# RWKV chunk inverse: transpositions on VectorE and block products on TensorE in place of round trips through DRAM; squares and low parts moved in the opening

## The chip, the cores and the metric

The kernel runs on one core of one Trainium2 chip. The time is the device time of one execution, in microseconds (us). In what follows PE is TensorE (the matrix engine), DVE is VectorE, ACT is ScalarE, POOL is GpSimd and SP is SyncE, which here only issues DMAs. PEld is PE's loading of stationary operands, beside its matmuls.

## The reference

Two layers over 256 tokens of width 1024. Each layer is a half-step SwiGLU network, three token mixers side by side (differential attention, RWKV-7, HGRN2), whose outputs are gated and summed, and a second SwiGLU half-step. The part that the change touches is the RWKV recurrence, over 8 heads of width 64:

```python
def step(state, inp):
    r_t, w_t, k_t, v_t, kk_t, a_t = inp
    s_kk = jnp.einsum('bhvk,bhk->bhv', state, kk_t)
    state = (state * w_t[:, :, None, :]
             - s_kk[..., None] * (kk_t * a_t)[:, :, None, :]
             + v_t[..., None] * k_t[:, :, None, :])
    return state, jnp.einsum('bhvk,bhk->bhv', state, r_t)
```

and, at the very start, the first sub-layer's norm: `u = modulate(rms_norm(h, norm_w[l, 0]), m[0], m[1])`, where m comes from the conditioning vector through the matrix mod_w.

## The kernel before, in words

**Weights.** All projections read fp32 weights from HBM in tiles of 512 KB ("weight tiles" below). `load` brings one into `raw`, ACT rounds it to `wh` (L375), and DVE makes the rest `wl = raw - wh` (L376). Activations have such pairs too (uh and ul, zh and zl). A product is three matmuls: wh with the high half, wh with the low half, wl with the high half. `mm3` (L372) makes 24 matmuls of 256 columns from a tile; the projections whose rows are tokens make 12 of 512 (L952, L953, L954). wh and wl have three buffers each, raw four.

**Order.** The main loop goes through the weight tiles in a fixed list (`items`, ORDER, BUDGET). Before each tile `advance` steps through the "tracks", Python generators that issue the mixers' own work piece by piece: each `yield` names the cost of the piece, a negative one ends the track's turn for this tile. Within these bounds a scheduler sets the order of each engine's instructions at build time, by priorities (PRIO) and dependencies; `pin` keeps an instruction in the order of the program. An engine runs its list in order, and waits where the next instruction is not ready.

**RWKV.** Time is cut into four chunks (c) of 64 tokens, and in each the recurrence is solved with the inverse of a unit triangular 64x64 matrix, for 8 heads: 4 pairs (j) by 2 (p). `rwkv_pair` fills H with these matrices, s on partitions. `rwkv_rest` (before: L776) inverts all 32.
- It takes the two 32x32 blocks on each diagonal (q = 0, 1) and moves them through DRAM (scrA, L782 and L788) to lie one block to a partition: NT, 64 partitions, and a copy on the other 64.
- The recursion (L799 a product, L801 a sum, for t = 1 to 15) inverts the two 16x16 blocks in each at once, in the free dimension.
- Four operations over 2048 elements make the 16x16 block below the diagonal (L808, L811, L813, L816).
- The result Y returns through DRAM (scrY, L821 to L827) into Ys, with s on partitions again.
- DVE transposes the upper blocks (Xa, L837), and two rounds of small matmuls (L841, L847) make the 32x32 blocks off the diagonal.
- The loop over c follows: pR (L864), pU with the inverse in Ys (L873), the state pS (L882) and the output pO (L896, L900). The norm of the output begins at L917.

HGRN2's track runs beside it; its small matmuls are L1016 and its DVE products write hw and PX.

**Opening.** The first layer's norm and its first six weight tiles run tile by tile, t = 0 to 7 (L1358 to L1382): two `mw` tiles of mod_w come in and DVE reduces them (L324) to `modd` (L328) and `mods` (L340); ACT makes zf from h and modd (L1366), DVE copies two columns into it (L1367), `split` makes zh on ACT and zl on DVE, and PE multiplies what is there of zf with the first raw tiles in plain fp32 (L1376). The squares of h (`z_square`, ACT L420) are added up on POOL (acc, L422), and after t = 4 two matmuls sum them (L433) and DVE takes the reciprocal root (nst, L380 to L385). POOL also builds masks there (blk, lmf), for `constants`.

Of the kernel before, what the change touches and what calls it, by code (L numbers as in the profile page):

```python
# [63 lines left out]
def trunk(ctx: ExitStack, tc: tile.TileContext, A, out):  # L64
# [36 lines left out]
    id32 = cp.tile([128, 32], F32, name="id32")  # L101
    omu = cp.tile([128, L, 15], F32, name="omu")
# [21 lines left out]
    def constants():  # L124
# [26 lines left out]
        for i, n in enumerate(LV):  # L151
# [263 lines left out]
    def z_square(k):  # L415
# [4 lines left out]
        SC.activation(sq, h[k], AF.Square)  # L420
# [128 lines left out]
    scr = drp.tile([2, 2, 16, 32, 32], F32, name="scrA")  # L549
    scy = drp.tile([2, 2, 16, 32, 32], F32, name="scrY")  # L550
# [3 lines left out]
    def mixer(l):  # L554
# [218 lines left out]
        def rwkv_rest():  # L773
# [12 lines left out]
            TM = hp.tile([128, 2048], F32, name="TM", tag="ZH")  # L786
# [3 lines left out]
            GP.memset(Y.rearrange("m a b -> m (a b)")[:, 0:1024:33], 1.0)  # L790
            yield 0.1
# [11 lines left out]
            Yh = tile_([128, 8, 16], "Yh", "rnt")  # L803
            PT = tile_([128, 8, 16], "PT", "rny")
# [665 lines left out]
```

## Time and profile before

| | us |
|---|---|
| three runs, median (lowest to highest) | 1449.73 (1449.04 to 1454.76) |
| the profiled execution | 1454.69 |
| its span | 1453.0 |
| PE busy | 1401.6 (96%) |
| DVE busy | 1184.9 (82%) |
| ACT busy | 803.3 (55%) |
| POOL busy | 150.2 (10%) |
| start of the first L372 matmul, behind the opening | 50.33 |

PE's mean granted clock is 0.988 of full speed (1.0 is 2.4 GHz, 0.5 is 1.2 GHz). A line of the profile's groups reads: line of the kernel, engine, operation, output from inputs by their names in the program, shapes, count; then the busy time and the mean ns of one; then the idle time of the engine just before these instructions and what ended it. Matmul records of plain fp32 (not of the rounded halves) stand twice in the trace.

### The profile page before, as it was taken

What the parts mean: (1) busy time and instruction counts of PE and PEld (TensorE: products, weight loads), DVE (VectorE), ACT (ScalarE), POOL (GpSimd) and SP (SyncE); (2) the same over time, 40 slices, a digit from 0 to 9 for tenths busy, and PEclk for the clock granted to TensorE, in tenths of its full rate; (3) what the DMA queues carried; (4) which work ended last, traced back from release to release, by engine and by line L of the source; (5) the groups of instructions that cost most, each with busy time, mean ns of one, the idle gap of its engine ahead of it and who ended that gap; (6) DMA issues with size and microseconds to landing.
All of it is one profiled execution on the core that took longest, in us unless ns stands there. A gap on an engine that the chain in (4) does not pass through costs nothing. (4 is left out here: it accounts for less than half of the span.)

```text
span 1453.0 us, 31223 instructions
## 1 busy us (share of the span) xinstructions
PE 1401.6 (96%) x12420; PEld 1331.2 (92%) x12420; DVE 1184.9 (82%) x2216; ACT 803.3 (55%) x1374; POOL 150.2 (10%) x251
## 2 busy tenths in 40 slices
PE   4999999999899999999999999999989999999999
PEld 3899999998678899999999999999877789999998
DVE  5999988869679999888879898787797788886553
ACT  2575447874255646554545544588534664665542
POOL 6200010031310021000000000100322001100000
PEclk9999999999799999999999999999999999999999
DMA  9769984455415657899878998544552235665564
GB/s 358 264 241 362 322 311 167 146 160 163 130 60 178 201 183 264 291 332 319 303 251 296 351 344 299 191 143 144 182 165 78 76 129 174 202 220 192 198 194 127
DMA packets 90370, 316.51 MB, mean 218 GB/s; under 512 B 10608, under 2 KB 13040, under 8 KB 90224
## 3 DMA queue, kind: packets, MB, share of 16 engines
q1 hardware_dynamic: 86832, 308.84, 62.0%
q0 software_dynamic: 1600, 4.20, 1.1%
q8 instruction: 97, 1.59, 0.4%
q10 hardware_dynamic: 1792, 1.48, 0.4%
q14 instruction: 49, 0.40, 0.1%
HBM read 312.38 MB, written 2.10 MB: 216 GB/s over the span
## 5 line engine op out<-in xcount | busy, mean ns | idle before, releaser
L375 ACT CAST wh<-raw 128x1024 fp32r<-128x1024 f32 (+1 forms) x440 | 455.5, 1036 | 426.9 <-PE psd L372 237.3
L376 DVE TENSOR_TENSOR wl<-raw,wh 128x1024 fp32r<-128x1024 f32 (+1 forms) x440 | 537.2, 1222 | 110.7 <-ACT wh L375 106.6
L372 PE MATMUL psd<-uh,wl 128*128 128x256 f32 x1664 | 228.9, 279 | 6.5 <-DVE wl L376 6.5
L372 PE MATMUL psd<-uh,wh 128*128 128x256 f32 x1664 | 231.4, 280 | 0.0
L372 PE MATMUL psd<-ul,wh 128*128 128x256 f32 x1664 | 227.1, 278 | 0.0
L372 PEld LDWEIGHTS psd<-uh,wl 128*128 128x128 f32 x1664 | 207.2, 189 | 8.2 <-DVE wl L376 7.7
L372 PEld LDWEIGHTS psd<-uh,wh 128*128 128x128 f32 x1664 | 207.7, 188 | 5.0 <-issue 2.7
L372 PEld LDWEIGHTS psd<-ul,wh 128*128 128x128 f32 x1664 | 206.4, 188 | 0.4
L324 DVE SCALAR_TENSOR_TENSOR mw<-mw,cbc 128x1024 f32<-128x1024 f32 x134 | 168.2, 1257 | 1.7 <-DMA mw<-in_modw 1.6
L372 PE MATMUL psd<-hl,wh 128*128 128x256 f32 x704 | 96.8, 278 | 0.0
L372 PE MATMUL psd<-hh,wl 128*128 128x256 f32 x704 | 96.6, 278 | 0.0
L372 PE MATMUL psd<-hh,wh 128*128 128x256 f32 x704 | 96.3, 277 | 0.0
L422 POOL TENSOR_TENSOR acc<-acc,sq 128x256 f32<-128x256 f32 x36 | 31.1, 865 | 575.1 <-ACT sq L420 443.6
L372 PEld LDWEIGHTS psd<-hl,wh 128*128 128x128 f32 x704 | 87.9, 188 | 0.0
L372 PEld LDWEIGHTS psd<-hh,wl 128*128 128x128 f32 x704 | 87.9, 188 | 0.0
L372 PEld LDWEIGHTS psd<-hh,wh 128*128 128x128 f32 x704 | 87.7, 188 | 0.0
L953 PE MATMUL psd<-wl,uh 128*128 128x512 f32 x160 | 66.5, 416 | 3.8 <-DVE wl L376 3.8
L954 PE MATMUL psd<-wh,ul 128*128 128x512 f32 x160 | 67.3, 421 | 0.0
L952 PE MATMUL psd<-wh,uh 128*128 128x512 f32 x160 | 66.0, 414 | 0.0
L372 PE MATMUL psd<-zh,wh 128*128 128x258 f32 x448 | 65.2, 286 | 0.0
L372 PE MATMUL psd<-zh,wl 128*128 128x258 f32 x448 | 64.9, 283 | 0.0
L372 PE MATMUL psd<-zl,wh 128*128 128x258 f32 x448 | 63.9, 283 | 0.0
(428 smaller groups left out, 2032.3 us busy)
## 6 DMA issues: line engine op xcount, KB each, us to landing
raw<-in_gu SPq DMA_DIRECT2D x176, 512.0 KB, 4.7
mw<-in_modw SPq DMA_DIRECT2D x134, 512.0 KB, 5.5
raw<-in_wfm SPq DMA_DIRECT2D x94, 512.0 KB, 3.3
raw<-in_dn SPq DMA_DIRECT2D x64, 512.0 KB, 4.7
raw<-in_wtm SPq DMA_DIRECT2D x40, 512.0 KB, 3.3
raw<-in_dn SPq DMA_DIRECT2D x32, 384.0 KB, 4.4
raw<-in_wo SPq DMA_DIRECT2D x24, 512.0 KB, 3.3
raw<-in_wout SPq DMA_DIRECT2D x16, 512.0 KB, 3.3
```

Source lines behind the costliest of these rows:

```text
L324: ins = V.scalar_tensor_tensor(w, w, 1.0, NOW["cbc"], ALU.mult, ALU.mult, accum_out=modd[:, l, j, f:f + 1])
L372: PE.matmul(p, w[:, sl[k]], xs[k][x], start=first and i == 0, stop=last and i == 3 * n - 1)
L375: SC.copy(dst_h, src)
L376: V.tensor_sub(dst_l, src, dst_h.bitcast(F32))
L422: GP.tensor_add(NOW["acc"], NOW["acc"], sq)
L952: PE.matmul(ps[b], u[k][0][:, ts_], w1, start=k == 0, stop=False)
L953: PE.matmul(ps[b], u[k][0][:, ts_], w2, start=False, stop=False)
L954: PE.matmul(ps[b], u[k][1][:, ts_], w1, start=False, stop=k == KT - 1)
```

## The change

The inverse no longer leaves the chip. H's diagonal 32x32 blocks are gathered into Hd, block m of the four partition quarters side by side. DVE's transposition, which works on 32x32 blocks, puts the 16 matrices of a quarter and their two halves g on the 32 partitions (To). `half`, a new constant of two columns (1 on the first and on the last 16 of every 32 partitions), picks the right half of each: NT is one 16x16 block to a partition, on 128 partitions, and the recursion runs over one block instead of two. A second transposition brings the result back (Yd, masked by `half` into two diagonal blocks), a third gives Xa, and two rounds of 64 matmuls of 32x32 make the block off the diagonal (L831, L837 of the changed kernel). Ys is filled by four copies. The older two rounds follow as L849 and L856, with p now in the inner loop. The four operations over 2048 elements and all DMAs of scrA and scrY are gone.

In the opening the squares of tiles 2t-2 and 2t-1 are made at step t, behind zh, and pinned there; zl of tile t-1 is made at step t, behind the two copied columns of zf; z_sums takes sq ahead of acc.

```diff
+            if n == 16:
+                V.tensor_reduce(half[:, 0:1], lmf[:, 1], AX.X, ALU.max)
+                V.tensor_scalar(half[:, 1:2], half[:, 0:1], -1.0, 1.0, ALU.mult, ALU.add)
...
-        for i, sq in enumerate((NOW["acc"], NOW["sq"])):
+        for i, sq in enumerate((NOW["sq"], NOW["acc"])):
...
-            for q in range(2):
-                for p in range(2):
-                    r0 = 64 * p + 32 * q
-                    GP.dma_start(scr[q, p].rearrange("m s t -> s m t"),
-                                 H[r0:r0 + 32, :, :, 32 * q:32 * q + 32].rearrange("s j c t -> s (j c) t"))
-            NT = tile_([128, 32, 32], "NT", "r")
-            Y = tile_([128, 32, 32], "Y", "k")
-            for d in range(2):
-                GP.dma_start(NT[64 * d:64 * d + 64], scr.rearrange("q p m s t -> (q p m) s t"))
+            quad = [slice(32 * i, 32 * i + 32) for i in range(4)]
+            Hd = tile_([128, 16, 32], "Hd", "Xa")
+            for i, r in enumerate(quad):
+                (GP.tensor_copy if i % 2 else SC.copy)(
+                    Hd[r].rearrange("s (j c) t -> s j c t", j=4), H[r, :, :, 32 * (i % 2):32 * (i % 2) + 32])
+            NT = tile_([128, 16, 16], "NT", "r")
+            Y = tile_([128, 16, 16], "Y", "k")
+            V.transpose(To.rearrange("p t (g m) -> p t g m", g=2), Hd.rearrange("p m (g t) -> p t g m", g=2))
+            GP.memset(Bd[:, :, 0:16], 0.0)
+            SC.activation(Bd[:, :, 16:32], Hd[:, :, 16:32], AF.Copy, scale=half[:, 0:1])
+            SC.activation(NT, To[:, :, 0:16].rearrange("p t s -> p s t"), AF.Copy, scale=half[:, 0:1])
+            V.scalar_tensor_tensor(NT, To[:, :, 16:32].rearrange("p t s -> p s t"), half[:, 1:2], NT, ALU.mult, ALU.add)
...
             for t in range(1, 16):
-                tm = TM[:, 0:2 * t * t].rearrange("m (g j s) -> m g j s", g=2, j=t)
-                V.tensor_tensor(tm, ap(Y, 0, [[528, 2], [32, t], [1, t]]), ap(NT, t, [[528, 2], [0, t], [32, t]]),
-                                ALU.mult)
-                V.tensor_reduce(ap(Y, t, [[528, 2], [32, t]]), tm, AX.X, ALU.add)
-                yield 0.2 + 4 * t * t / 960.0
+                tm = TM[:, 0:t * t].rearrange("m (j s) -> m j s", j=t)
+                V.tensor_tensor(tm, ap(Y, 0, [[16, t], [1, t]]), ap(NT, t, [[0, t], [16, t]]), ALU.mult)
+                V.tensor_reduce(ap(Y, t, [[16, t]]), tm, AX.X, ALU.add)
+                yield 0.4 + 2.7 * t * t / 960.0
...
-            tm = TM.rearrange("m (j t s) -> m j t s", j=8, t=16)
-            V.tensor_tensor(tm, Yh.unsqueeze(2).to_broadcast([128, 8, 16, 16]),
-                            ap(NT, 16, [[0, 8], [1, 16], [32, 16]]), ALU.mult)
-            V.tensor_reduce(PT, tm, AX.X, ALU.add)
-            V.tensor_tensor(tm, PT.unsqueeze(2).to_broadcast([128, 8, 16, 16]),
-                            ap(Y, 528, [[0, 8], [1, 16], [32, 16]]), ALU.mult)
-            V.tensor_reduce(Yh, tm, AX.X, ALU.add)
...
-            GP.dma_start(sm[:, 0:8], Y[0:64, 0:8])
...
+            V.transpose(To.rearrange("p t (g m) -> p t g m", g=2),
+                        Y.rearrange("p s t -> p t s").unsqueeze(2).to_broadcast([128, 16, 2, 16]))
+            for g in range(2):
+                SC.activation(Yd[:, :, 16 * g:16 * g + 16], To[:, :, 16 * g:16 * g + 16].rearrange("p t m -> p m t"),
+                              AF.Copy, scale=half[:, g:g + 1])
+            V.transpose(Xa, Yd)
+            for m in range(16):
+                for i, r in enumerate(quad):
+                    PE.matmul(p1[r, m], Bd[r, m], Xa[r, m], start=True, stop=True, tile_position=(32 * i, 32 * i))
+            SC.copy(Tt, p1)
+            for m in range(16):
+                for i, r in enumerate(quad):
+                    PE.matmul(p2[r, m], Tt[r, m], Yd[r, m], start=True, stop=True, tile_position=(32 * i, 32 * i))
+            V.tensor_tensor(Yd[:, :, 16:32], Yd[:, :, 16:32], p2[:, :, 16:32], ALU.add)
+            for i, r in enumerate(quad):
+                (GP.tensor_copy if i % 2 else SC.copy)(Ys[r, :, 32 * (i % 2):32 * (i % 2) + 32], Yd[r])
+            V.transpose(Xa, Yd)
+            yield -1.0
...
-        split(zh[:, t], zl[:, t], zf[:, t])
+        if t:
+            pin(V.tensor_sub(zl[:, t - 1], zf[:, t - 1], zh[:, t - 1].bitcast(F32)))
+        SC.copy(zh[:, t], zf[:, t])
+        if 0 < t < 5:
+            for k in (2 * t - 2, 2 * t - 1):
+                z_square(k, pin)
...
-            for k in range(KT):
-                z_square(k)
```

Three places show how the instructions move. The first is DVE in the first layer, around the last steps of the inverse; the wl rows are those of the weight tiles. Before:

```order
L808 TENSOR_TENSOR TM<-Yh,NT 128x2048
L376 TENSOR_TENSOR wl<-raw,wh 128x1024
L811 TENSOR_REDUCE PT<-TM 128x128
L376 TENSOR_TENSOR wl<-raw,wh 128x1024
L813 TENSOR_TENSOR TM<-PT,Y 128x2048
L376 TENSOR_TENSOR wl<-raw,wh 128x1024
L816 TENSOR_REDUCE Yh<-TM 128x128
L376 TENSOR_TENSOR wl<-raw,wh 128x1024
L818 COPY Y<-Yh 64x8x16
L819 COPY Y<-Yh 64x8x16
```

and now, from the recursion's last step on:

```order
L812 TENSOR_TENSOR TM<-Y,NT 128x225
L813 TENSOR_REDUCE Y<-TM 128x15
L381 TENSOR_TENSOR wl<-raw,wh 128x1024
L816 STREAM_TRANSPOSE To<-Y 128x512
L1030 TENSOR_TENSOR sd<-psm,id_90 128x256
L381 TENSOR_TENSOR wl<-raw,wh 128x1024
L827 STREAM_TRANSPOSE Xa<-AI 128x512
L381 TENSOR_TENSOR wl<-raw,wh 128x1024
```

Where four long operations stood between the wl rows, there are two transpositions. The recursion also begins four tiles earlier: its first step stands behind the 91st wl of the kernel, before behind the 95th.

The second place is PE in the first layer, from the first block product to the chunk loop. Before:

```order
L953 MATMUL psd<-wl,uh_3046 128x512
L841 MATMUL psm<-Xa,H 32x32 x16
L954 MATMUL psd<-wh,ul_3047 128x512
L952 MATMUL psd<-wh,uh_3046 128x512
L953 MATMUL psd<-wl,uh_3046 128x512
L954 MATMUL psd<-wh,ul_3047 128x512
L841 MATMUL psm<-Xa,H 32x32 x16
L847 MATMUL psm<-Ys,Tt 32x32 x16
L1016 MATMUL psm<-hw,hk 32x32 x28
L847 MATMUL psm<-Ys,Tt 32x32 x16
L1016 MATMUL psm<-hw,hk 32x32 x4
L864 MATMUL psm<-SV,Za 64x64 x4
```

Now the first product, and the start of the weight tile behind it (24 rows of L377 in all):

```order
L963 MATMUL psd<-wl,uh_3149 128x512
L964 MATMUL psd<-wh,ul_3150 128x512
L1026 MATMUL psm<-hw,hk 32x32 x32
L831 MATMUL psm<-Xa,AI 32x32 x64
L377 MATMUL psd<-uh_2897,wh 128x256
```

The groups L831, L837, L849 and L856, then those of the chunk loop, each stand behind one whole weight tile now; before they stood within some two tiles.

The third place is DVE in the opening, at t = 5, where the reciprocal root (nst) is made. Before:

```order
L437 TENSOR_SCALAR nst<-psm 128x2
L328 TENSOR_SCALAR modd<-modd,mb_105,cols 128x1
L380 TENSOR_SCALAR nst<-nst 128x2
L324 SCALAR_TENSOR_TENSOR mw,modd<-mw,cbc 128x1024
L381 TENSOR_SCALAR nst<-nst 128x2
L340 TENSOR_TENSOR mods<-modd,cols 128x1
L383 SCALAR_TENSOR_TENSOR nst<-nst 128x2
L1367 COPY zf<-mods 128x2
```

and now:

```order
L442 TENSOR_SCALAR nst<-psm 128x2
L333 TENSOR_SCALAR modd<-modd,mb_106,cols 128x1
L385 TENSOR_SCALAR nst<-nst 128x2
L166 TENSOR_REDUCE half<-lmf 128x1
L386 TENSOR_SCALAR nst<-nst 128x2
L329 SCALAR_TENSOR_TENSOR mw,modd<-mw,cbc 128x1024
L388 SCALAR_TENSOR_TENSOR nst<-nst 128x2
L167 TENSOR_SCALAR half<-half 128x1
L345 TENSOR_TENSOR mods<-modd,cols 128x1
L389 TENSOR_TENSOR nst<-nst 128x2
L173 TENSOR_SCALAR omu<-cols 128x15
L1377 COPY zf<-mods 128x2
```

`half` reads POOL's mask lmf there, and thirteen more constants (omu, hka, oka, hwa, hm, he) follow among the nst rows. On POOL the six additions of acc, which stood between the first masks, now stand in one block ahead of blk and lmf.

## Rows read from the trace of the kernel before

**Rows 1.** PE's waits over the whole span: us in total, times, longest us.
```profile
PE psd L1376 <- DVE zf L1367: 13.9, 4, 11.5
PE psd L372 <- DVE wl L376: 6.5, 6, 2.0
```

**Rows 2.** Windows of the two stretches: busy us by engine, PEclk, DMA share, GB/s.
```profile
343.30:422.17 78.87, 72.28 (x1082) 61.29 (x1080) 62.61 (x80) 33.23 (x57) 20.85 (x25) 0.87 0.35 113
1052.80:1129.00 76.20, 70.09 (x1082) 59.20 (x1080) 63.65 (x81) 33.25 (x57) 20.59 (x25) 0.91 0.36 117
```

**Rows 3.** The same view, finer, in the first layer.
```profile
343.00:370.00 27.00, 21.91 (x237) 20.75 (x236) 26.75 (x25) 11.22 (x18) 4.38 (x7) 0.99 0.42 142
380.00:396.00 16.00, 16.00 (x297) 13.17 (x295) 7.87 (x13) 4.20 (x7) 1.11 (x2) 0.50 0.31 91
```

**Rows 4.** Groups of PE's instructions from 343.3 to 422.17: busy, mean ns, idle before.
```profile
L372 PE MATMUL psd<-uh,wl 128*128 128x256 f32 x72 | 10.7, 286 | 3.2 <-DVE wl L376 3.2
L953 PE MATMUL psd<-wl,uh 128*128 128x512 f32 x16 | 7.9, 496 | 1.9 <-DVE wl L376 1.9
L873 PE MATMUL psm<-R,Ys 64*64 64x64 f32 x64 | 4.3, 250 | 0.0
L1016 PE MATMUL psm<-hw 128*32 128x32 f32 x256 | 3.6, 210 | 0.0
L841 PE MATMUL psm<-Xa,H 32*32 32x32 f32 x64 | 3.1, 214 | 1.0 <-DVE Xa L837 1.0
```

**Rows 5.** Timeline of PE: start us, us, instruction, count; idle before it in brackets.
```profile
346.14 0.76 PE L1016 MATMUL psm<-hq,hk 128*32 128x32 f32 x64
346.83 1.18 PE L372 MATMUL psd<-uh,wh 128*128 128x256 f32 x8
347.85 1.07 PE L372 MATMUL psd<-ul,wh 128*128 128x256 f32 x8
348.76 0.96 PE L372 MATMUL psd<-uh,wl 128*128 128x256 f32 x7
...
378.18 1.17 PE L841 MATMUL psm<-Xa,H 32*32 32x32 f32 x32 [1.03 <-DVE Xa L837]
379.27 0.50 PE L954 MATMUL psd<-wh,ul 128*128 128x512 f32 x1
...
400.31 0.68 PE L873 MATMUL psm<-R,Ys 64*64 64x64 f32 x16
400.93 0.51 PE L954 MATMUL psd<-wh,ul 128*128 128x512 f32 x1
```

**Rows 6.** Timeline of DVE, first layer: recursion, 2048-element operations, first transposition.
```profile
328.11 1.23 DVE L376 TENSOR_TENSOR wl<-raw,wh 128x1024 fp32r<-128x1024 f32 x1 [1.52 <-ACT wh L375]
329.25 0.15 DVE L799 TENSOR_TENSOR TM<-Y,NT 128x2 f32<-128x2 f32 x1
329.44 0.16 DVE L801 TENSOR_REDUCE Y<-TM 128x2 f32<-128x2 f32 x1
...
352.82 4.04 DVE L808 TENSOR_TENSOR TM<-Yh,NT 128x2048 f32<-128x2048 f32 x1
...
366.20 2.29 DVE L816 TENSOR_REDUCE Yh<-TM 128x128 f32<-128x2048 f32 x1
...
377.33 0.70 DVE L837 STREAM_TRANSPOSE Xa<-Ys 32x512 f32<-32x512 f32 x1 [0.51 <-DMA Ys<-scrY]
```

**Rows 7.** The opening: SP's and DVE's timeline, and the landing times of mw.
```profile
12.82 0.81 SPq L323 DMA_DIRECT2D mw<-in_modw  x2
...
DMA to landing us min/median/max: 5.2/7.5/8.6
...
21.33 0.43 DVE L376 TENSOR_TENSOR zl<-zf,zh 128x258 fp32r<-128x258 f32 x1 [3.52 <-ACT zh L375]
21.68 1.22 DVE L324 SCALAR_TENSOR_TENSOR mw<-mw,cbc 128x1024 f32<-128x1024 f32 x1
...
29.27 0.43 DVE L376 TENSOR_TENSOR zl<-zf,zh 128x258 fp32r<-128x258 f32 x1 [0.53 <-ACT zh L375]
```

More of the change, by code (lines that the diff above doesn't have):

```diff
@@ L101, in trunk @@
     id32 = cp.tile([128, 32], F32, name="id32")
+    half = cp.tile([128, 2], F32, name="half")
     omu = cp.tile([128, L, 15], F32, name="omu")
@@ L413, in z_tile, with z_square @@
         z_square(k)
-    def z_square(k):
+    def z_square(k, keep=lambda i: i):
         if k == 0:
@@ L419, in z_square @@
             sq = tp.tile([128, S], F32, name="sq", tag="sqz")
-        SC.activation(sq, h[k], AF.Square)
+        keep(SC.activation(sq, h[k], AF.Square))
         if 0 < k < KT - 1:
@@ L546, in ffn @@
                 add(A["dn"][l, i, f][:, k0 * 128:(k0 + kn) * 128], kn * 128, partial(down, f, k0, kn))
-    scr = drp.tile([2, 2, 16, 32, 32], F32, name="scrA")
-    scy = drp.tile([2, 2, 16, 32, 32], F32, name="scrY")
     c3 = lambda t: t.rearrange("p (c t) -> p c t", t=C)
@@ L815, in rwkv_rest @@
-            yield 2.2
-            V.tensor_reduce(Yh, tm, AX.X, ALU.add)
-            yield -2.2
-            V.tensor_copy(Y[0:64, 0:8, 16:32], Yh[0:64])
-            V.tensor_copy(Y[64:128, 8:16, 16:32], Yh[64:128])
-            sm = scy.rearrange("q p m s t -> (q p m) s t")
-            GP.dma_start(sm[:, 0:8], Y[0:64, 0:8])
-            GP.dma_start(sm[:, 8:16], Y[64:128, 8:16])
-            GP.dma_start(sm[:, 16:32], Y[0:64, 16:32])
-            for q in range(2):
-                for p in range(2):
-                    r0 = 64 * p + 32 * q
-                    GP.dma_start(Ys[r0:r0 + 32, :, 32 * q:32 * q + 32], scy[q, p].rearrange("m s t -> s m t"))
@@ L831, in rwkv_rest @@
+            M["inv"] = True
+            yield -0.7
+            for g in range(2):
+                SC.activation(Yd[:, :, 16 * g:16 * g + 16], To[:, :, 16 * g:16 * g + 16].rearrange("p t m -> p m t"),
+                              AF.Copy, scale=half[:, g:g + 1])
+            yield -0.1
             Xa = tile_([128, 16, 32], "Xa")
@@ L833, in rwkv_rest @@
             p1 = psm([128, 16, 32])
+            V.transpose(Xa, Yd)
+            yield -0.6
+            for m in range(16):
+                for i, r in enumerate(quad):
+                    PE.matmul(p1[r, m], Bd[r, m], Xa[r, m], start=True, stop=True, tile_position=(32 * i, 32 * i))
+            SC.copy(Tt, p1)
+            yield -0.2
+            p2 = psm([128, 16, 32])
+            for m in range(16):
[6 more added lines that the diff above has]
+            yield -1.0
+            p1 = psm([128, 16, 32])
             p2 = psm([128, 16, 32])
             hv = [(slice(64 * p, 64 * p + 32), slice(64 * p + 32, 64 * p + 64)) for p in range(2)]
-            for a_, b_ in hv:
-                V.transpose(Xa[a_], Ys[a_, :, 0:32])
-            yield -1.2
-            for p, (a_, b_) in enumerate(hv):
-                for m in range(16):
+            for m in range(16):
+                for p, (a_, b_) in enumerate(hv):
                     PE.matmul(p1[b_, m], H[a_, m // 4, m % 4, 32:64], Xa[a_, m], start=True, stop=True,
                               tile_position=(64 * p, 64 * p + 32))
+            for p, (a_, b_) in enumerate(hv):
                 SC.copy(Tt[b_], p1[b_])
             yield -0.2
+            for m in range(16):
+                for p, (a_, b_) in enumerate(hv):
+                    PE.matmul(p2[a_, m], Tt[b_, m], Yd[b_, m], start=True, stop=True,
+                              tile_position=(64 * p + 32, 64 * p))
             for p, (a_, b_) in enumerate(hv):
-                for m in range(16):
-                    PE.matmul(p2[a_, m], Tt[b_, m], Ys[b_, m, 32:64], start=True, stop=True,
-                              tile_position=(64 * p + 32, 64 * p))
                 V.tensor_copy(Ys[a_, :, 32:64], p2[a_])
@@ L1382, in trunk @@
             z_rstd()
+    V.tensor_sub(zl[:, KT - 1], zf[:, KT - 1], zh[:, KT - 1].bitcast(F32))
     for i in range(NI, len(items) + AHEAD):
```

19 lines of the change are left out of this document (9 added, 10 removed).

## The prediction

> **What bounds the kernel now.** I read the page's busy shares first (in the table above): PE is busy for 1401.6 of 1453.0 us, so only what shortens PE's stream, or the gaps in it, moves the end. Second, PE's waits over the whole span [rows 1]. The reader is to see how short they are: the largest is the opening's wait for zf, and behind it come the 6.5 us for wl, the low halves of the weights. Third, I cut out in each layer the thirteen weight tiles from the end of the inverse's recursion to the RWKV norm [rows 2]. They take 78.87 and 76.20 us, and PE's granted clock there is 0.87 and 0.91 of full speed, while it is 0.988 over the whole span. Cut finer [rows 3], it is 0.99 from 343 to 370 us and 0.50, the lower level of 1.2 GHz, all through 380 to 396. What PE did as it fell: at 378.18 it had idled 1.03 us for Xa [rows 5], then ran the two block products L841 and L847 and the first chunks' 64-wide products with few weight tiles between them.
>
> What would the first stretch take with nothing lost? I count its matmul records [rows 4] and price each kind at the upper clock [rows 5].
> - 216 of 256 columns (three operand pairs of L372, 72 each): from 347.85 to 348.76 eight take 0.91 us, 0.114 each: 24.6 us.
> - 49 of 512 columns (L953, with L952 and L954): twice that, 0.2275 each: 11.1.
> - 304 of 64 columns (L873 and L896 64 each, L882 48, L864 and L900 64 each): sixteen take 0.62 us from 400.31 to 400.93, 38.8 ns each: 11.8.
> - 384 small ones of L1016, 256 of them in one row: 64 in 0.69 us from 346.14, 10.8 ns each: 4.1.
> - 128 of L841 and L847: 32 in 1.09 us from 378.18, 34 ns each: 4.4.
>
> Sum: 56.0 us. The stretches take 22.9 and 20.2 us more. Of the first, 6.1 are waits (3.2 + 1.9 + 1.0, the idle times in [rows 4]), (1 - 0.87) x 78.87 = 10.3 are the clock, and some 6.5 go to changes between kinds of matmul. The room lies where the inverse's end crowds the stream.
>
> **The change, part by part.** *The inverse on DVE.* Four operations over 2048 elements go, the first and the last of them in [rows 6]; two products of 4.0 and two sums of 2.3 are 12.6 us per layer, one wl tile between each two. They hold wl back, which is most of PE's 6.1 us. The recursion is halved; where it ran PE hardly waited, so that by itself is worth nothing; it lets the end come sooner. New are four transpositions of 512 elements per partition, priced like L837 at 0.70: 2.8 us. What is late next? In the changed order DVE does from its first new transposition to its third 8 wl (1.23 each: 9.8), three transpositions (2.1), the assembly of NT (0.7, priced like one), seven HGRN products of 512 elements (the same price: 4.9) and the recursion. That has 1240 products now, at (4.04 - 0.15)/2048 = 1.9 ns, and their sums at (2.29 - 0.15)/2048 = 1.05, so 3.7 us, and 30 operations that start 0.19 apart when they are small: 5.7. Together 26.9 us. PE needs 8 x 3 x 0.91 = 21.8 for the tiles and 1.4 for two groups of L1016: 23.2. DVE falls 3.7 us behind, and three wl buffers let it be ahead by up to two tiles. I keep 3 us of waits per layer, between 0 (the lead covers it) and 6 (nothing gained).
>
> *The DRAM round trips.* POOL's DMAs and their latency go. PE sees of them the 1.0 us for Xa and the delay of what follows. ACT and POOL get four copies each instead; where they are late, PE does other tiles, and the price is in the 3 us.
>
> *The block products.* PE gets 64 + 64 matmuls of 32x32 per layer, 256 records, since the trace holds each of these twice (L841: 32 in the program, 64 in its row). They go round four tile positions. The nearest row is L1016, small ones on several positions: 256 x 10.8 ns = 2.8 us. The other is L841, sixteen in a row on one position, 34 ns: 8.7 us. I take 2.8, because the new loops have the position innermost. By the Trainium skill's page "TensorE: Matmul & The Clock Gate", section "Wait — 56ns, not 53.3ns?", matmuls never start closer than about 25 ns however narrow they are, which would make it an estimated 6.4 us; L1016's record stands at 10.8 ns, so the measurement decides. L841's and L847's successors now alternate between two positions: 128 x 34 / 2 = 2.2 us saved, at worst 0.
>
> *The spacing.* The new order puts each group of the inverse and of the first chunks behind a whole weight tile, where they were packed. That makes about 22 breaks in the stream. After a break eight matmuls take 1.02 us (346.83 to 347.85) instead of 0.91; I count the 0.11 twice, for the way in as well: 4.8 us, between 2.4 and 8. In return the packed band at the lower clock goes; I forecast the upper clock throughout.
>
> Sum per stretch: 56.0 + 2.8 - 2.2 + 4.8 + 3 = 64.4 us, which saves 14.5 and 11.8: 26.3.
>
> *The opening.* ACT now makes the squares behind zh, and DVE makes zl(t-1) only behind the zf of t, so that it no longer waits for ACT. The wait of 3.52 us at 21.33 [rows 7] looks large. But the next mw tile, which DVE takes at 21.68, was issued at 12.82, and these land 7.5 us after issue at the median, so about 20.5: near 1 us is left to gain there, and 0.53 at each of three later tiles: 2.5. Against that, the order puts some 15 small operations (half, omu, hka ...) into the chain of the rsqrt, ahead of the last mw tiles, at 0.16: 2.4. L166 moreover waits for POOL's first mask, which now stands behind six additions of acc. I take 0 for the opening, between -5 (all of DVE's waits for zh that arrivals don't cover, and the smaller operations hidden) and +3 (the mask is late).
>
> Total: 1454.69 (the profiled execution; 1.69 of it lie outside the span) - 26.3 = **1428.4 us**. The profiled execution is 4.96 above the median of 1449.73. Its first stretch has more of the lower clock than its second; if the median run has both like the second, it goes from 1449.73 by 2 x 11.8 to 1426.1. I predict **1428**.
>
> **The rivals.**
> - *The small groups are dear.* The 256 cost 34 ns, not 10.8: 5.9 us more per layer, 1440.2. For it: L841 is the only row of that shape. Against: it stood on one tile position, and the change goes round four. By the skill's 25 ns, named above, it would be an estimated 1435.6.
> - *DVE becomes the wait.* The recursion and its transpositions run between wl tiles that PE wants every 2.73 us, with strided reads that no row prices. If the 3.7 us above become 9, PE waits 5 more per layer: 1438.4, or 1441.4 with a bad opening. For: wl is already the wait in the stretches. Against: 12.6 us of DVE work are gone.
> - *The clock does not come back.* The small matmuls themselves bring it down, not their crowding, and the 10.3 and (1 - 0.91) x 76.20 = 6.9 us stay lost: 1428.4 + 17.2 = 1445.6. For: the fall begins with small groups. Against: [rows 3] has 0.99 where groups of L1016 stand between weight tiles.
> - *Slower.* The same mechanism spread: breaks behind every tile keep PE at 1.2 GHz through the whole tail. Each us at the lower clock loses half a us, so 72 us in the two layers give 1428.4 + 36 = 1464. It is slower by over 0.5% from about 57 us on. For: some 22 breaks more, and twice the 32-wide products. Against: the 0.99 from 343 to 370, again.
>
> **How the numbers follow.** 0.5% is 7.2 us, about what a measurement of this kernel can tell from no change: faster means under 1442.5, slower over 1457. The forecast (1417 to 1436) gets 0.60, better still through the opening 0.04, dear groups 0.12, DVE 0.11, the clock 0.08 (a quarter of it under 1442.5), slower 0.05. Faster: 0.60 + 0.04 + 0.12 + 0.10 + 0.02 = 0.88, less 0.02 for two rivals at once: 0.86; same 0.09; slower 0.05. The range: below, 1428.4 less the 6 us of waits kept and 5 of the opening, 1417, and 1415 from the median's lower start; above, it takes in dear groups and DVE, each with a bad opening, to 1443. Some 15 in 100 lie outside.
>
> **What would show it.** Right: the idle times for wl and Xa in each stretch fall from 6.1 to about 3 us; the same thirteen tiles take about 64 us at a clock above 0.97; L831's and L837's groups of 128 records take about 1.4 us. The regular matmuls start at about 50.3 us as before. Wrong: a new wait of PE for wl while the recursion runs, groups that take over 4 us, slices at a clock of 0.50 for longer than 16 us, or a start of the regular matmuls over 3 us from 50.3.

## The result, and the profile after

The changed kernel takes **1433.36 us** (median of four runs, 1429.65 to 1436.48), the kernel before 1450.43 on the same chip (four runs, 1449.04 to 1454.76): a ratio of 0.9873, with an interval of 0.9849 to 0.9897. It was forecast at 1428, so 5 us too low, and within the range. The profiled execution after is the fastest of its four (1429.65) and the one before the slowest of its own (1454.69): the two traces differ by 25.0 us, the medians by 17.1. So some 8 of the 25 us that are divided up below lie between executions and are not the change.

PE and DVE on the page after, against 1401.6 and 1184.9 us before:

```profile
span 1427.9 us, 32229 instructions
PE 1382.9 (97%) x12932; PEld 1316.9 (92%) x12932; DVE 1156.3 (81%) x2210; ACT 809.6 (57%) x1392; POOL 144.7 (10%) x235
```

Where the 25 us came from is read from windows that start and end at the same weight tiles in both kernels (columns as in [rows 2]). Before: the first network, the eighteen tiles from the start of the first layer's recursion to its RWKV norm, the rest of that layer's mixers, the networks between the mixers, and the second layer's two windows:

```profile
50.33:237.41 187.08, 186.32 (x1572) 185.80 (x1571) 171.81 (x346) 104.51 (x160) 8.04 (x9) 1.00 0.83 296
329.57:422.94 93.37, 86.78 (x1145) 73.25 (x1144) 75.82 (x107) 40.62 (x66) 23.51 (x27) 0.89 0.37 119
422.94:552.08 129.14, 125.27 (x971) 114.01 (x969) 114.79 (x292) 74.33 (x164) 10.67 (x11) 1.00 0.56 181
552.08:946.92 394.84, 391.70 (x3392) 390.23 (x3391) 341.13 (x563) 210.26 (x312) 15.07 (x19) 1.00 0.85 294
1039.07:1129.78 90.71, 84.60 (x1146) 71.17 (x1144) 76.86 (x107) 40.65 (x66) 23.25 (x27) 0.92 0.38 123
1129.78:1257.28 127.50, 125.39 (x971) 114.20 (x969) 106.10 (x271) 76.04 (x167) 8.73 (x11) 1.00 0.42 141
```

After, the same:

```profile
48.70:230.28 181.58, 181.58 (x1572) 181.27 (x1571) 171.00 (x330) 101.32 (x158) 9.83 (x17) 1.00 0.86 305
322.74:410.86 88.12, 82.33 (x1449) 70.49 (x1448) 59.00 (x90) 45.08 (x77) 19.35 (x16) 0.98 0.38 125
410.86:541.07 130.21, 125.01 (x922) 113.26 (x921) 114.29 (x292) 70.94 (x156) 11.36 (x11) 0.97 0.55 181
541.07:931.50 390.43, 390.16 (x3393) 389.51 (x3392) 340.59 (x563) 210.09 (x312) 16.28 (x22) 1.00 0.86 298
1023.93:1109.83 85.90, 80.77 (x1450) 68.98 (x1449) 58.92 (x90) 45.09 (x77) 19.36 (x16) 1.00 0.39 128
1109.83:1233.01 123.18, 121.25 (x922) 110.71 (x921) 105.52 (x270) 72.30 (x158) 9.77 (x11) 1.00 0.44 146
```

The two stretches with the inverse, where I put the whole gain, became 5.3 and 4.8 us shorter. The first network gained 5.5 and the networks between the mixers 4.4, where nothing of the inverse runs, and the opening ended 1.6 earlier (48.70 against 50.33). Behind the stretches the second layer gained 4.3 and the first lost 1.1; the rest adds up to 0.2. So of the 25 us of this pair the mixers gave 13.3, and the opening and the networks some 12.

That is one pair of executions. In a second profiled execution of the change (e3, below, the slowest of its six) the mixers' four windows are 88.16, 130.89, 90.05 and 126.65 us, only 5.0 us shorter than before. Its second layer:

```profile
1027.93:1117.98 90.05, 83.68 (x1449) 71.81 (x1448) 59.04 (x90) 45.19 (x77) 19.11 (x16) 0.96 0.38 123
1117.98:1244.63 126.65, 124.79 (x923) 113.33 (x921) 105.87 (x270) 72.51 (x158) 10.10 (x11) 0.97 0.43 142
```

The clock came back for the most part: 0.98 and 1.00 in the stretches against 0.89 and 0.92 (0.98 and 0.96 in e3). But PE still waited in them, 5.8 and 5.1 us by the two windows, where I had kept 3. PE's waits over the whole span after, to be set beside [rows 1]; the first three of these lines are the stretches', but for 1.7 us of L963:

```profile
PE psd L963 <- DVE wl L381: 5.7, 7, 1.7
PE psm L1026 <- issue: 4.6, 2, 2.6
...
PE psm L874 <- DVE SV L901: 2.2, 2, 1.1
...
PE psm L438 <- ACT sq L425: 0.3, 1, 0.3
```

The second line is a wait that the kernel before had for 0.2 us only (at L847). Its place in the first layer:

```profile
340.40 0.76 PE L1026 MATMUL psm<-hw,hk 128*32 128x32 f32 x64
341.10 1.29 PE L831 MATMUL psm<-Xa,AI 32*32 32x32 f32 x128
342.31 1.22 PE L377 MATMUL psd<-uh,wh 128*128 128x256 f32 x8
...
345.34 1.29 PE L837 MATMUL psm<-AI,Tt 32*32 32x32 f32 x128
346.56 0.32 PE L1026 MATMUL psm<-hw 128*32 128x32 f32 x12
349.53 0.96 PE L1026 MATMUL psm<-hw 128*32 128x32 f32 x52 [2.65 <-issue]
350.42 2.08 PE L377 MATMUL psd<-uh,wh 128*128 128x256 f32 x8
...
358.58 1.20 PE L856 MATMUL psm<-AI,Tt 32*32 32x32 f32 x64
359.71 0.76 PE L1026 MATMUL psm<-hw 128*32 128x32 f32 x64
```

The 128 block products cost 1.22 us (345.34 to 346.56, 9.5 ns a record), as forecast. But PE stops for 2.65 us in the middle of a group of 64 like matmuls, after the twelfth, with no engine or DMA as releaser. Right behind it eight matmuls take 1.87 us: the granted clock is 0.50.

### The profile page after: what moved, and what is told of

Its sections match the earlier page's. It is cut to its first block, busy times and chain, and to the rows that moved or that the text cites. A ratio compares the mean times of both kernels' runs of the same rounds, so it can differ in the third digit from the quotient of the medians.

```text
span 1427.9 us, 32229 instructions
## 1 busy us (share of the span) xinstructions
PE 1382.9 (97%) x12932; PEld 1316.9 (92%) x12932; DVE 1156.3 (81%) x2210; ACT 809.6 (57%) x1392; POOL 144.7 (10%) x235
## 3 DMA queue, kind: packets, MB, share of 16 engines
q8 instruction: 101, 1.65, 0.5%
## 4 chain that ended last, share of the span: by engine, by line
PE 77%; DVE 10%; ACT 7%; issue 2%; DMA 2%; SPq 0%; POOL 0%; DVEq 0%; ACTq 0%
PE psd L377 65%; DVE wl L381 4%; ACT wh L380 2%; PE psd L963 1%; PE psd L962 1%; PE psd L964 1%; DMA h<-in_x 1%; DVE TM L812 1%; ACT ae L1216 1%; DMA mw<-in_modw 1%; DVE mw L329 1%; PE psm L1026 1%; PE psm L678 0%; PE psm L752 0%; PE psm L906 0%
## 5 line engine op out<-in xcount | busy, mean ns | idle before, releaser
L377 PE MATMUL psd<-uh,wh 128*128 128x256 f32 x1664 | 233.1, 281 | 0.0
L377 PE MATMUL psd<-uh,wl 128*128 128x256 f32 x1664 | 227.1, 278 | 1.8 <-DVE wl L381 1.8
L377 PE MATMUL psd<-ul,wh 128*128 128x256 f32 x1664 | 227.6, 278 | 0.0
L377 PEld LDWEIGHTS psd<-uh,wh 128*128 128x128 f32 x1664 | 208.0, 189 | 5.2 <-issue 2.0
L377 PEld LDWEIGHTS psd<-uh,wl 128*128 128x128 f32 x1664 | 206.1, 188 | 3.1 <-DVE wl L381 2.2
L377 PEld LDWEIGHTS psd<-ul,wh 128*128 128x128 f32 x1664 | 206.2, 188 | 0.5
L377 PE MATMUL psd<-hh,wh 128*128 128x256 f32 x704 | 95.5, 276 | 0.0
L377 PE MATMUL psd<-hh,wl 128*128 128x256 f32 x704 | 95.4, 276 | 0.0
L377 PE MATMUL psd<-hl,wh 128*128 128x256 f32 x704 | 95.4, 276 | 0.0
L377 PEld LDWEIGHTS psd<-hh,wh 128*128 128x128 f32 x704 | 87.0, 188 | 0.0
L377 PEld LDWEIGHTS psd<-hh,wl 128*128 128x128 f32 x704 | 86.9, 188 | 0.0
L377 PEld LDWEIGHTS psd<-hl,wh 128*128 128x128 f32 x704 | 86.9, 188 | 0.0
L963 PE MATMUL psd<-wl,uh 128*128 128x512 f32 x160 | 65.6, 410 | 5.7 <-DVE wl L381 5.7
L377 PE MATMUL psd<-zh,wh 128*128 128x258 f32 x448 | 65.3, 287 | 0.0
L377 PE MATMUL psd<-zh,wl 128*128 128x258 f32 x448 | 64.8, 283 | 0.0
L377 PE MATMUL psd<-zl,wh 128*128 128x258 f32 x448 | 63.9, 283 | 0.0
```

The source lines that it names most:

```text
L377: PE.matmul(p, w[:, sl[k]], xs[k][x], start=first and i == 0, stop=last and i == 3 * n - 1)
L963: PE.matmul(ps[b], u[k][0][:, ts_], w2, start=False, stop=False)
```

## The experiments

Each median stands beside that of the same chip's runs of the kernel before. e1 to e4 ran on one chip, e5 to e8 on a second, e9 to e11 on a third, e12 on a fourth; a trace is one execution.

**e1, the inverse alone.** The opening's edits are undone.

```diff
-        for i, sq in enumerate((NOW["sq"], NOW["acc"])):
+        for i, sq in enumerate((NOW["acc"], NOW["sq"])):
...
-        if t:
-            pin(V.tensor_sub(zl[:, t - 1], zf[:, t - 1], zh[:, t - 1].bitcast(F32)))
-        SC.copy(zh[:, t], zf[:, t])
+        split(zh[:, t], zl[:, t], zf[:, t])
```

> The new inverse with the opening of before. Theory: by the item times of the two profiled executions the opening saved 1.63 us (50.33 to 48.70) and the RWKV part some 5 us per layer, so this kernel takes 1433.4 + 1.6 = 1435 us. Rival: the opening's saving is chance or is given back further on; then it takes 1433.4. In both cases its two RWKV stretches look like those of the changed kernel, with the two gaps of PE in the L1026 groups (2.65 and 1.99 us).

1448.33 against 1450.50, ratio 0.9986 (0.9972 to 1.0001): nothing left of the gain, where both theories had expected 1433 to 1435. The regular matmuls start at 55.69 in place of 50.33, for a reason in the waits of the first 60 us (us in total, times, longest):

```profile
DVE half L166 <- POOL lmf L159: 7.0, 1, 7.0
```

`half` waits on DVE for POOL's mask, with the `mw` tiles queued behind it. The late mask that I had given +3 costs 5 without the opening's edits; with them it costs nothing.

**e2, the opening alone.** The inverse of the kernel before with the new opening, and no `half`.

```diff
-        for i, sq in enumerate((NOW["acc"], NOW["sq"])):
+        for i, sq in enumerate((NOW["sq"], NOW["acc"])):
...
-        split(zh[:, t], zl[:, t], zf[:, t])
+        if t:
+            pin(V.tensor_sub(zl[:, t - 1], zf[:, t - 1], zh[:, t - 1].bitcast(F32)))
+        SC.copy(zh[:, t], zf[:, t])
...
```

(against the kernel before)

> The new opening with the inverse of before. Theory: 1450.4 - 1.6 = 1448.8 us, first L372 matmul at about 48.7 us, because DVE no longer waits for zh. Rival: the opening is bounded by the arrival of the mw tiles, and its regular matmuls start within 0.5 us of 50.33; then 1450.4. Third: without the constants in the rsqrt chain (they are moved in the changed kernel only as its scheduler puts them) it starts earlier still, at 46 to 48, and the time is 1446 to 1448.

1443.74 against 1450.50, 0.9950 (0.9931 to 0.9968): 6.8 us, where I had expected under 2 (4.4 at most, for a start at 46 to 48). The start is at 49.74, 0.6 earlier, and the first network takes 181.38 us as in the change, 5.7 less than in the trace before. PE's waits name one more part. Before, for the sums of squares:

```profile
PE psm L433 <- POOL acc L422: 4.4, 5, 1.6
```

In e2 1.1 us of this are left (for `sq`), in the change 0.3, in e1 6.0: the exchanged order in `z_sums`, one line of the diff, lets PE multiply ACT's last square while POOL ends the sum. At the norms behind the opening's nothing else of the opening's edits differs.

**e3, the change again**, on this chip, with no edit.

> The changed kernel once more, for a second trace and more times. Theory: of the 25 us between the two profiled executions some 8 are not the change: in the execution of before, matmuls of 256 columns started 117.5 ns apart from 103 to 222 us, though nothing waited and the clock was full, and 113.7 ns apart in the changed kernel. If that is an execution's own state, this one shows 117.5 in some stretches of the feed-forward networks, and takes 1432 to 1437. Rival: it belongs to the kernel before (to its order of work); then this trace has 113.7 in the same stretches again, and the time stays at 1430.

1437.12 against 1450.50, 0.9901 (0.9879 to 0.9923), 13.4 us. The same gap stands at the same record, twelve behind L837, 2.63 us; in the second layer it is 3.24 us where it was 1.99, with the granted clock at 0.50 for 6.8 us behind it, and for 6.8 us again from 1129.3. The first network takes 181.60 us, so the slower pace of the trace before (last section) was not met again; but the time did not stay at 1430, as the rival had it. This execution is 12.0 us longer than the one above: 8.3 in the mixers, 1.9 in the networks between them, 1.2 at the start.

**e4, the block products cut in two**, each half behind a weight tile of its own.

```diff
             for m in range(16):
+                if m == 8:
+                    yield -0.3
```

(in both rounds, L831 and L837 of the change)

> Each of the two 64-matmul groups L831 and L837 cut in two, a weight tile between the halves. Theory (instruction supply): PE's gaps in the middle of the L1026 group, 2.65 and 1.99 us, come from the program's code arriving too slowly, since two groups of 128 records each run at 9.5 ns a record; with half the density the gaps fall under 0.5 us, the slices at the lower clock from 349 to 353 us go, and the time falls by 4.6 + 1.7 less four more breaks at 0.2 = 5.5, to 1428. Rival (data): L1026 waits for an event of another engine that the profile does not show; then the gaps stay, and the time rises by about 1 us to 1434.

1427.35 against 1450.50, 0.9837 (0.9812 to 0.9861), 9.8 us under the change on the same chip. The gap is gone in the first layer, 0.65 us of it is left in the second, and the half clock behind it is gone too. No dependency was taken away, and two breaks more in each layer were added.

**e5, the first round twice**, 256 records where 128 stood.

```diff
-            for m in range(16):
+            for m in [*range(16)] * 2:
```

> The changed kernel with the 64 matmuls of L831 issued twice (the same result). PE's own work grows by 1.2 us per layer. Theory (instruction supply): the second 64 use up what has been fetched, so PE's gaps without a releaser grow from 4.6 to 5.9 us in the two layers to 8 us or more, and begin earlier, in L837 or in L831 itself; time 1435 + 2.4 + 3 or more, 1440 to 1445. Rival (data): the gaps stay in L1026 at 4.6 to 5.9 us, and the time is 1437.5.

1441.73 against 1450.30, 0.9938 (0.9914 to 0.9961). The added records alone would be 1.2 us per layer. PE's timeline in the second layer:

```profile
1045.83 0.76 PE L1026 MATMUL psm<-hw,hk 128*32 128x32 f32 x64
1046.52 1.60 PE L831 MATMUL psm<-Xa,AI 32*32 32x32 f32 x166
1050.84 0.97 PE L831 MATMUL psm<-Xa,AI 32*32 32x32 f32 x90 [2.72 <-issue]
...
1054.77 0.32 PE L837 MATMUL psm<-AI,Tt 32*32 32x32 f32 x14
1055.41 1.17 PE L837 MATMUL psm<-AI,Tt 32*32 32x32 f32 x114 [0.32 <-issue]
1056.51 0.32 PE L1026 MATMUL psm<-hw 128*32 128x32 f32 x13
1058.97 0.65 PE L1026 MATMUL psm<-hw 128*32 128x32 f32 x51 [2.15 <-issue]
```

The gap now stands inside L831, whose operands were all there, and two more follow. From the first to the second PE does 90 + 24 + 14 = 128 matmul records (the 24 are the weight tile, whose rows are left out above), from the second to the third 114 + 13 = 127. A wait for data would not count matmuls. In the first layer the gap is 4.01 us, after 165 records.

**e6, one tile position after the other**: the loops exchanged in both rounds, sixteen matmuls in a row on one position.

```diff
-            for m in range(16):
-                for i, r in enumerate(quad):
+            for i, r in enumerate(quad):
+                for m in range(16):
```

> L831 and L837 with the tile position in the outer loop, 16 matmuls in a row on one position. Theory (position): a record then takes 34 ns as in L841 of before, so each group takes 4.35 us instead of 1.2; four groups are 12.5 us more. By the theory of instruction supply the gaps of 4.6 to 5.9 us go at the same time, since the code is used more slowly: net +7, 1442. Rival (the position's order does not matter): groups stay at 1.2 us, gaps stay, 1435. Second rival (gaps have another cause): groups at 4.35 us and gaps as they are, 1447.

1443.55 against 1450.30, 0.9953 (0.9932 to 0.9975). PE's timeline:

```profile
348.49 3.93 PE L837 MATMUL psm<-AI,Tt 32*32 32x32 f32 x128
352.35 0.76 PE L1026 MATMUL psm<-hw 128*32 128x32 f32 x64
```

3.86 us for the group, 30 ns a record, and no gap behind it: this is the rival "small groups are dear", made to happen, and it does cost what L841 told. In the second layer the long groups bring the half clock besides (0.63 from 1050 to 1064).

**e7 and e9, a late wl in the first network.** One `wl` at about 97 us is made again, once in e7, four times more in e9 (here), to see whether one late weight tile changes the pace of what follows.

```diff
+        if i == 20:
+            for _ in range(4):
+                V.tensor_sub(wl, raw, wh.bitcast(F32))
```

> The changed kernel with one wl of the first feed-forward network made twice, at about 90 us: 1.2 us more on DVE, once. The lead of wl over PE there is at least 0.96 us in the trace of the changed kernel, so PE loses some 0.2 us directly. Theory (a late operand leaves PE in a slower rhythm): behind the first late wl the matmuls of 256 columns start 117.5 ns apart instead of 113.7, as in the kernel before from 103.6 us on, until the next norm at some 222 us: 1100 x 3.8 ns = 4.2 us; the first network (first L372 matmul to the tile behind the norm) takes 186 us instead of 181.6, and the time rises by 4 to 5. Rival (the rhythm was a state of that execution): 113.7 ns stay, the time rises by 0.2 to 0.5.

> As the kernel with one wl made twice, but made five times: 4.6 us more on DVE at about 90 us, more than the lead of wl. (Made twice, it stayed covered, and said nothing on the question.) Theory (a late operand leaves PE in a slower rhythm): PE waits some 2 to 3 us for wl at 95 to 105 us, and from there to the norm at some 222 us matmuls of 256 columns start 117.5 ns apart; the first network takes 181.6 + 2.5 + 4 = 188 us, and the time is 1435 + 6.5. Rival (the rhythm was a state of that one execution): 181.6 + 2.5 = 184, 113.7 ns stay.

e7 took 1436.77 against 1450.30, 0.9915 (0.9887 to 0.9943): PE never waited, the first network is as in the change (181.61), so it tells nothing. e9 took 1442.66 against 1450.60, 0.9953 (0.9936 to 0.9971), its first network 189.66 us, 8.1 more. Its PE timeline at the wait, and 32 us later:

```profile
98.15 1.76 PE L377 MATMUL psd<-uh,wl 128*128 128x256 f32 x13 [2.90 <-DVE wl L1357]
...
130.54 1.11 PE L377 MATMUL psd<-uh,wh 128*128 128x256 f32 x8
131.48 1.10 PE L377 MATMUL psd<-ul,wh 128*128 128x256 f32 x8
```

The waits for wl are 3.1 us in that network. The other 5.0 are nowhere a wait: eight matmuls take 0.94 to 0.95 us instead of 0.907, from about 121 us to the network's end. The long wait did not set that pace by itself: behind it eight matmuls still take 0.907 us up to 118. The slower pace begins at 121.24, behind a hold of 0.11 us where wl had come 0.05 us before its group.

**e8 and e10, POOL's product for HGRN moved.** In the change it runs beside the end of the recursion (below). e8 issues it at the fourth level of HGRN's own loop and leaves the place to the scheduler, e10 (here) pins it there; both stand on e4.

```diff
-                GP.tensor_mul(h4(gw[:, b]), h4(gw[:, b]),
-                              row(l, "hgn", 0, 128).unsqueeze(1).to_broadcast([128, 4, 128]))
...
+                    if n == 4:
+                        gw = M["hgw"]
+                        for b in range(2):
+                            g3 = gw[:, b].rearrange("p (h d) -> p h d", h=4)
+                            pin(GP.tensor_mul(g3, g3, row(l, "hgn", 0, 128).unsqueeze(1).to_broadcast([128, 4, 128])))
```

> The kernel with the groups cut in two (1427.35 us), and POOL's two multiplications of hgw by a weight row moved from the recursion's last steps, where a wl of 2.32 us (others 1.22) and a recursion product of 1.21 (others of its size 0.5) stand beside them, to HGRN's fourth level. Theory (POOL slows DVE while both run): the wl wait of 1.4 us at that place goes in both layers, with the slower rhythm behind it: 1.4 x 2 + some 1 = 3 to 4 us, 1424. Rival (DVE has too much work there whoever runs beside it): the wait stays above 1 us and the time stays at 1427; or the wait turns up at the new place.

> The kernel with the groups cut in two, with POOL's two multiplications of hgw held at HGRN's fourth level by the order of the program (without that the scheduler had put them back to the old place, and the trace of that kernel had the same wl of 2.31 us and the same wait of 1.36 us). Theory (POOL slows DVE while both run): the wl beside them goes back from 2.31 to 1.22 us and the product of 196 from 1.21 to 0.5; PE's wait of 1.4 us at about 335 and 1033 us goes, 3 to 4 us in all, 1424. Rival (DVE has too much work there): wl stays at 2.3 us or the wait stays above 1 us, 1427.

e8 took 1427.47 against 1450.30, 0.9848 (0.9824 to 0.9872), like e4: the scheduler put the product back (at 330.78), so it tells nothing. e10 took **1422.54** against 1450.60, 0.9808 (0.9792 to 0.9824), 4.8 us under e4, which ran on another chip. DVE in the change, two consecutive instructions of the recursion's end:

```profile
331.42 1.21 DVE L812 TENSOR_TENSOR TM<-Y,NT 128x196 f32<-128x196 f32 x1
332.56 2.32 DVE L381 TENSOR_TENSOR wl<-raw,wh 128x1024 fp32r<-128x1024 f32 x1
```

POOL in the change, at the same time:

```profile
330.99 2.81 POOL L1002 TENSOR_TENSOR hgw<-hgw,rows 128x512 f32<-128x512 f32 x2 [12.34 <-DVE hgw L1001]
```

And the same two instructions of DVE in e10:

```profile
331.50 0.50 DVE L812 TENSOR_TENSOR TM<-Y,NT 128x196 f32<-128x196 f32 x1
331.93 1.21 DVE L381 TENSOR_TENSOR wl<-raw,wh 128x1024 fp32r<-128x1024 f32 x1
```

Beside POOL's two products DVE's took 0.71 and 1.11 us longer, 1.8 together. The wait of 1.4 us for the next wl, in each layer, went with them, and the half clock is nowhere left in the mixers. Their four windows are now 82.61, 127.84, 82.48 and 124.41 us, 23.4 shorter than before. By the Trainium skill's page "SBUF — State Buffer", section "SBUF: two separate sides", the two engines share a pair of ports that one operation holds to its end, which the other waits for where it reads two operands from SBUF; both of DVE's do, and the trace agrees (0.71 and 1.11 us longer beside POOL's).

**e11 and e12, `half` made late**, from another mask at the end of `constants`: e11 is the inverse alone as in e1, e12 is e10 with this edit.

```diff
-            if n == 16:
-                V.tensor_reduce(half[:, 0:1], lmf[:, 1], AX.X, ALU.max)
...
+        lm16 = tp.tile([128, 32], F32, name="lm16", tag="nt", bufs=1)
+        pin(V.tensor_copy(lm16, lmask[:, 0]))
+        V.tensor_reduce(half[:, 0:1], lm16, AX.X, ALU.max)
```

> The new inverse with the opening of before, and the constant half made from a mask after the opening instead of in it. In the trace of the new inverse with the old opening, DVE waited 7.0 us for POOL's mask before L166, and the first L372 matmul stood at 55.69 us. Theory: that wait is the whole reason why the inverse alone gained nothing; here the regular matmuls start at 50.3 us and the time is 1448.3 - 5.4 = 1443 us, 7 below before. Rival: the inverse is worth nothing by itself whatever the opening does; then the start moves to 50.3 but the time stays above 1447.

> The fastest kernel so far (groups cut in two, POOL's multiplications held back: 1422.54 us) with half made from a mask after the opening; with it the thirteen other constants leave the opening's rsqrt chain too. It tests the term of the prediction that put 2.4 us on these operations. Theory of that term: they stand on the path to the last zf, and the first L372 matmul comes 1.5 to 2.5 us earlier than 48.8; time 1420.5. Rival: they fill pauses of DVE between dependent small operations (in the trace of the changed kernel the nst rows with them in between start 0.07 apart, without them 0.2), so that the start moves under 0.5 us; time 1422.5. Second rival: in the first feed-forward network they make a wl late, and the slower rhythm costs 4 us: 1426.

e11 took 1445.25 against 1450.60, 0.9957 (0.9937 to 0.9978): without the wait for the mask (start at 50.39) the inverse alone is worth 5.3 us, between what the two theories had said. e12 took 1427.54 against 1452.43, 0.9836 (0.9802 to 0.9870): no gain over e10, and none of the three expected times. The small constants are out of the chain of the reciprocal root there. But from `nst` to `nv` DVE takes 4.19 us (36.54 to 40.73) with no such operation between, against 4.20 in the change (34.48 to 38.68) with them. They fill pauses. That its regular matmuls start at 51.05, later than with the constants, lies ahead of this chain, where nst waits 3.46 us for PE's sums (1.91 in the change); the cause of that wait was not looked for. The second rival, a slower pace, is not met: the first network takes 181.58 us.

## Why the prediction was right, and where it wasn't

**The time was right, in part by luck.** Forecast was a gain of 26.3 us, all in the stretches with the inverse, and 0 in the opening. By e2 the opening's edits alone give 6.8, by e11 the inverse alone gives 5.3, both together 13.4 to 17.1. In the profiled pair the mixers gained 13.3 us, in e3's trace 5.0: the inverse's term was two to five times too large, and one for the opening and the networks was missing. That the sum came within 5 us of the median (9 in e3) is luck as far as these two make up for each other. The mechanism holds where nothing else is in its way: without PE's gap and POOL's product the mixers are 23.4 us shorter than before in e10's trace and 22.2 in e12's.

**The inverse on DVE: right.** The 2048-element operations are gone, DVE's busy time in the first stretch fell from 75.82 to 59.00 us. "Three us behind" was too kind: wl was late once by 1.4 us in each layer, through POOL, which the prediction didn't look at (e10).

**The block products: right.** The group goes at 9.5 ns a record, within 2.8 us per layer, and L849 and L856, on two positions, at 17.7 (64 in 1.13 us from 358.58), so 128 x (34 - 17.7) = 2.1 us saved against the 2.2 forecast. The 25 ns between starts that the prediction cited from the Trainium skill's page "TensorE: Matmul & The Clock Gate", section "Wait — 56ns, not 53.3ns?", don't hold here. The rival "dear" falls; e6 shows under which order of the loops it would have come true.

**The waits, 3 us per stretch: the step that failed.** It asked only who was late with data, and put the supply of PE's instructions at nothing. The first stretch waited 5.8 us, of which 2.65 for a block of instructions (last section), and the half clock behind that gap lost another 1.7. Measured without gap and POOL's product (e10), the waits are 2.0.

**The sum of the stretch.** Forecast were 14.5 and 11.8 us less, so 78.9 us for either window of eighteen tiles; measured 88.1 and 85.9. Of the 9.2 missing in the first layer, 2.8 are the waits, 1.7 the clock, and another 2.8 no loss at all: twelve matmuls of L678, four of L927 and 32 of L1061 now lie inside the window and not behind it (1.25 + 0.91 from 408.38 to 410.54, and 0.63). About 2 remain, in both layers, and are the breaks between kinds of matmul, which I had at 4.8 us. In the second layer it is 2.1 + 0 + 2.8 + 2. What moved in was gained behind the window there; in the first layer the half clock took it back (from 448.4 for 6.8 us, with waits for wl of 1.8 and 1.7 that end at 447.5 and 450.5).

**The clock: right for the packed band, too hopeful for the rest.** The 17.1 us at 0.50 [rows 3] are gone. The rivals "does not come back" and "slower" fall. But 10.2 us at the lower level stay in the mixers of the profiled execution, all in the first layer, and 23.8 in both layers of e3, against 34.1 before; in e10 there are none.

**The opening, 0: mis-sized.** The gain at the start was forecast at 2.5 and is 1.6 in the profiled pair, where executions differ as much: with the change's opening the regular matmuls start at 48.45 to 50.30 us in nine traces, with the old one at 50.33 (before) and 50.39 (e11). The 2.4 set against it for the small constants are 0 (e12, from nst to nv). Not priced at all was the order in `z_sums`: PE's waits for these sums are 4.4, 6.0 and 4.9 us in the three traces with the old order (before, e1, e11) and 0.3 to 1.6 in the eleven with the new. Nor was PE's pace in the first network. That network took 187.08 us in the trace before, but 183.95 in e1 and 183.44 in e11, whose opening is the old one too, and 181.4 to 181.6 in the ten traces with the new opening that have no wl made late on purpose. So 1.8 to 5.7 us are the opening's, the waits for the sums included, and the 5.5 of the pair is near the upper end.

## What to carry to other kernels

Price small matmuls by the number of tile positions they go round, and then look at how many follow one another without a long one between: a run of over 128 records (64 plain fp32 matmuls of the program) can outrun its own instructions, and one weight tile between two halves is cheaper than the gap. An idle time of PE that ends inside a group of like matmuls, with no releaser, is a matter of supply and not of data; count the matmuls between two such gaps, and look for a packet of the instruction queue that ended just before PE went on. Divide up the difference of two traces only as far as a second trace of the same kernel repeats it. And when the diff has a side part that looks small, run it alone: here one exchanged pair in a loop took away 2.8 us of waits or more, while the small operations that I had counted beside it cost nothing.

## What was not expected of the hardware

**Instructions come in blocks.** The gaps of e5 lie 128 matmuls apart. The page counts the traffic of a queue for instructions. After, and with the old inverse (e2: 12420 matmuls and as many loads, after: 12932):

```profile
q8 instruction: 101, 1.65, 0.5%
```

```profile
q8 instruction: 97, 1.59, 0.5%
```

1.65 MB over 2 x 12932 instructions of PE are 64 bytes each, in e2 the same, and 25864 / 101 = 256 instructions to a packet: 128 matmuls and their loads. In 9.5 ns each these are gone in 1.2 us. With the gap behind it such a block took 1.2 + 2.65 us after, 3.2 to 5.2 in the gaps that follow such a group, which is then how long the next needs; 3.86 us of e6 cover it.

The trace also holds each packet of that queue with its time, and these settle the cause. For four of the gaps (us; the last column counts PE's matmul records ahead of the gap):

| gap of PE | PE stops | packet starts | packet ends | PE goes on | records |
|---|---|---|---|---|---|
| after, first layer, L1026 | 346.88 | 347.05 | 348.24 | 349.53 | 2888 |
| e8, first layer, L841 (L837 of the change) | 349.57 | 346.95 | 348.76 | 350.25 | 2888 |
| after, second layer, L1026 | 1047.96 | 1047.79 | 1048.75 | 1049.95 | 9379 |
| e5, second layer, L831 | 1048.12 | 1048.13 | 1049.34 | 1050.84 | 9380 |

Behind the opening, the traces of the change and of e1 to e12 have 19 gaps of 0.3 us or more with no releaser, 0.32 to 4.01 us long. Each ends 1.20 to 1.55 us after such a packet has ended, and the next packet starts 1.0 to 2.3 us after PE goes on. They stand at fixed records whatever instruction is there: in the first layer at 2888 or 2889 in eight traces (L1026, L841 of e8, L847 of the old inverse in e2) and one block earlier, at 2761, in e5; in the second at 9379 or 9380 in all eight that have one, with two more of e5 about a block apart behind it. So PE waits for the next block of its instructions. What sets the time of a packet's start was not looked for. The Trainium skill's page "Runtime: NRT & Kernel Launch", section "Instruction fetch mechanics", gives the same 256 instructions to a block, and holds their cost to be mostly hidden; here the gaps cost 4.6 us in the two layers, and the clock behind the first.

**A short hold can set a slower pace.** In the kernel before, PE's groups of eight at 100 us (columns as in [rows 5]):

```profile
102.48 1.07 PE L372 MATMUL psd<-ul,wh 128*128 128x256 f32 x8
103.39 1.15 PE L372 MATMUL psd<-uh,wl 128*128 128x256 f32 x8
104.38 1.10 PE L372 MATMUL psd<-uh,wh 128*128 128x256 f32 x8
105.32 1.11 PE L372 MATMUL psd<-ul,wh 128*128 128x256 f32 x8
```

After, the same tiles:

```profile
102.65 1.07 PE L377 MATMUL psd<-uh,wh 128*128 128x256 f32 x8
103.56 1.07 PE L377 MATMUL psd<-ul,wh 128*128 128x256 f32 x8
```

Starts lie 0.91 us apart after, all through the network; before they go from 0.91 to 0.94 at 103.39, where wl had only just come (it ended at 103.27), and stay there to about 222 us, at a granted clock of 1.00 and with no wait shown. e11, with the old opening too, has the same tile as late (wl ended at 103.52, its group starts at 103.58), and there the slower pace ends at 106.65, behind one more hold of 0.03 us:

```profile
104.62 1.11 PE L377 MATMUL psd<-uh,wh 128*128 128x256 f32 x8
105.56 1.11 PE L377 MATMUL psd<-ul,wh 128*128 128x256 f32 x8
...
107.46 1.07 PE L377 MATMUL psd<-uh,wh 128*128 128x256 f32 x8
108.36 1.07 PE L377 MATMUL psd<-ul,wh 128*128 128x256 f32 x8
```

So a short hold can start the slower pace and another can end it; in e9 a wait of 2.9 us left the pace as it was, and a hold of 0.11 us changed it. Which of the two paces follows a hold stays open.

**The fastest version** is e10: the change, its block products in two halves, POOL's product at a pinned place. 1422.54 us, 28 less than the kernel before. e12, the same but for `half`, took 1427.54 on another chip; its two stretches are as short (82.39 and 82.40 us against 82.61 and 82.48), its opening and the networks between the mixers were longer.
